# HGRN's value tiles: 32x32 block transposes on VectorE and a pass through DRAM in place of TensorE transposes

## The chip, the cores and the metric

One core of a Trainium2 chip runs the whole layer. The metric is device time in microseconds (us); the kernel before took 2657.88 us (median of three runs, 2653.09 to 2657.88). One more execution was recorded by the hardware profiler; all rows below are from that one.

## The reference

A hybrid decoder layer in float32 on 2048 tokens of width 1024. One projection feeds two groups of heads, HGRN2 (4 heads of 128) and RWKV-7 (8 heads of 64); their outputs go through one output projection, and a convolutional feed-forward follows.

```
h = rmsnorm(x)
hg_p, rw_p = split(h @ w_in)
q, f, v, g = split(hg_p, 4)          # HGRN2; v is what this change handles
f = lb + (1 - lb) * sigmoid(f);  q = silu(q) * 128**-0.5;  k = 1 - f
S_t = diag(f_t) S_{t-1} + k_t v_t^T;  o_t = S_t^T q_t
o_hg = rmsnorm_per_head(o) * norm_w * silu(g)
o_rw = rwkv7(rw_p)                   # S_t = S diag(w) + (S a) b^T + v k^T
x = x + concat(o_hg, o_rw) @ w_out
x = x + conv_ffn(rmsnorm(x))         # up, causal conv of width 3, silu gate, down
out = rmsnorm(x)
```

## The kernel before

The tokens are cut into four blocks of 512. The first stage (`phase1`) does the projections and both recurrences of all blocks; the second, which the change does not touch, does the last output projection and the feed-forward.

Everything in the first stage is kept with features on the 128 partitions and tokens along the free axis. A projection is 24 matmuls of 128x128 by 128x512 (each product of split operands takes three) into one of two `pj` banks, and an `ev_` function takes it out of the bank. For HGRN, `ev_q`, `ev_f`, `ev_v` and `ev_g` do so for a head `j` of block `nb`; there are 16 such units, (block, head). `ev_v` copies the bank with ScalarE into `hv` (two buffers): value features on partitions, 512 tokens along the row.

`hg_unit` then does the recurrence of a unit in chunks. It needs the values the other way round, tokens on partitions: `VT`, 128 x 4 x 128 with one buffer. Before, four TensorE transposes (L950) put the 128x128 blocks of `hv` into an `hg` bank and ScalarE copied them to `VT`. VT is read late in the unit: by the state update (L1053) and by the output (L1062). After that its buffer is used for a split half of the squared output (`part`).

RWKV works in `rw_super`, twice per block, on two pairs of heads. It makes products `M` (masked on VectorE at L733), stores the diagonal 32x32 blocks of them to DRAM in runs of 32 floats (`Ed`, L745), loads them back with one small matrix per partition (`E`, L748), and solves the triangular systems with a loop of 31 steps of two VectorE instructions (L800 and L802). The result `Ti` is turned with VectorE's block transpose (`TZ`, L806), and the matmuls at L819 take it up. This is called a solve below; there are eight.

The order of the work comes from three generators that are run in turn: one step of `rw_stream`, one step of `hg_stream`, then projection matmuls (`dense`) worth 2000 ns by the generator's own count. Each `yield` ends a step. The scheduler then settles each engine's order. On each engine instructions run in that order, and what an engine waits for holds up all that stands behind. SyncE issues the loads of x, the stores of oT, x1d and h2d, and RWKV's Ed and E; GpSimd issues the weights.

## Time and profile before

| | us |
|---|---|
| median of three runs | 2657.88 |
| lowest, highest | 2653.09, 2657.88 |
| the profiled execution | 2662.58 |
| its span, first to last instruction | 2660.8 |
| the first stage in it, from the first projections to the last output projection of block 2 | 30 to 1326 |

How to read the rows: PE is TensorE, PEld its weight loads, DVE VectorE, ACT ScalarE, POOL GpSimd, SP SyncE. A row of a group names line, engine, operation, output<-inputs, shape and count, then the busy time, the mean length of one in ns, the idle time of the engine just before and what ended it. A row of waits reads "who <- for whom: us in total, times, longest". A row of the timeline has start, length, engine, line, operation.

### The profile page before, as it was taken

The numbers are of one execution on the slowest core, as the hardware profiler recorded it, in microseconds if no ns is written. First come the engines' busy times: TensorE is split into PE (matmuls) and PEld (weight loads), VectorE is DVE, ScalarE is ACT, GpSimd is POOL, SyncE is SP. The second block draws the span as 40 slices with busy tenths as digits, with TensorE's granted clock in tenths as the row PEclk, the third lists the DMA queues.
The fourth block names the chain that finished last, engine by engine and source line by source line (L and its number), as shares of the span: only waits on it lengthen the run. The fifth ranks groups of instructions, "written<-read, shape, count | busy, mean of one in ns | idle before, by whom it ended". The sixth has DMA issues, their size and how long they took to land. (4 is left out here: it accounts for less than half of the span.)

```text
span 2660.8 us, 51050 instructions
## 1 busy us (share of the span) xinstructions
PE 2560.2 (96%) x19595; PEld 2061.2 (77%) x19595; DVE 1952.9 (73%) x3728; ACT 1389.2 (52%) x2274; POOL 380.4 (14%) x686
## 2 busy tenths in 40 slices
PE   7999999989999999999899999999999999999998
PEld 5777777766777777777678888887888887888887
DVE  4877667576567765767678789987998887766556
ACT  5566453545535555445456754456545544545444
POOL 6433222212222122222100000000000000000000
PEclk9999999999999999999999999999999999999999
DMA  8645443445643456744493468646763553998665
GB/s 303 204 165 170 158 143 120 130 148 203 199 143 126 156 196 199 276 131 136 154 309 113 143 204 266 233 154 225 245 203 131 166 189 127 327 320 286 197 191 186
DMA packets 312714, 510.59 MB, mean 192 GB/s; under 512 B 46879, under 2 KB 143509, under 8 KB 312469
## 3 DMA queue, kind: packets, MB, share of 16 engines
q1 hardware_dynamic: 257937, 328.99, 37.4%
q0 software_dynamic: 54464, 178.32, 20.4%
q8 instruction: 154, 2.52, 0.4%
q14 instruction: 91, 0.75, 0.1%
q10 hardware_dynamic: 68, 0.02, 0.0%
HBM read 372.99 MB, written 134.22 MB: 191 GB/s over the span
## 5 line engine op out<-in xcount | busy, mean ns | idle before, releaser
L270 PE MATMUL pj<-hh,wh 128*128 128x512 f32 x960 | 393.4, 410 | 6.2 <-ACT rkv L122 3.3
L271 PE MATMUL pj<-hl,wh 128*128 128x512 f32 x960 | 377.8, 394 | 1.3 <-issue 1.3
L272 PE MATMUL pj<-hh,wl 128*128 128x512 f32 x960 | 377.5, 393 | 0.0
L270 PE MATMUL ua<-Bh,uwh 128*128 128x512 f32 x704 | 276.4, 393 | 4.4 <-ACT m L122 3.1
L272 PE MATMUL ua<-Bh,uwl 128*128 128x512 f32 x704 | 274.6, 390 | 0.0
L271 PE MATMUL ua<-Bl,uwh 128*128 128x512 f32 x704 | 274.3, 390 | 0.0
L270 PEld LDWEIGHTS pj<-hh,wh 128*128 128x128 f32 x960 | 181.5, 189 | 55.2 <-issue 8.7
L272 PEld LDWEIGHTS pj<-hh,wl 128*128 128x128 f32 x960 | 181.1, 189 | 40.6 <-issue 1.7
L271 PEld LDWEIGHTS pj<-hl,wh 128*128 128x128 f32 x960 | 181.6, 189 | 34.3 <-DVE hl L488 0.5
L254 ACT CAST uwh<-uraw 128x512 fp32r<-128x512 f32 x220 | 134.2, 617 | 128.9 <-PE ua L271 55.7
L255 DVE TENSOR_TENSOR dal<-draw,dah 128x512 fp32r<-128x512 f32 x138 | 95.4, 691 | 113.4 <-ACT dah L254 113.2
L255 DVE TENSOR_TENSOR uwl<-uraw,uwh 128x512 fp32r<-128x512 f32 x220 | 147.6, 688 | 34.9 <-ACT uwh L254 34.8
L254 ACT CAST dah<-draw 128x512 fp32r<-128x512 f32 x138 | 85.7, 621 | 164.9 <-PE da L271 80.6
L270 PEld LDWEIGHTS ua<-Bh,uwh 128*128 128x128 f32 x704 | 132.2, 188 | 34.1 <-ACT m L122 5.7
L272 PEld LDWEIGHTS ua<-Bh,uwl 128*128 128x128 f32 x704 | 132.3, 188 | 28.1 <-DVE uwl L255 0.4
L271 PEld LDWEIGHTS ua<-Bl,uwh 128*128 128x128 f32 x704 | 132.3, 188 | 26.7
L270 PE MATMUL ud<-Bh,uwh 128*128 128x512 f32 x352 | 138.1, 392 | 0.0
L272 PE MATMUL ud<-Bh,uwl 128*128 128x512 f32 x352 | 137.2, 390 | 0.0
L271 PE MATMUL ud<-Bl,uwh 128*128 128x512 f32 x352 | 137.1, 390 | 0.0
L1493 POOL DMA_DIRECT2D gd<-y x2 | 1.1, 540 | 946.8 <-DVE y L1491 946.8
L271 PE MATMUL da<-dbl,dah 128*128 128x512 f32 x332 | 129.5, 390 | 0.2 <-DVE dbl L255 0.2
L272 PE MATMUL da<-dbh,dal 128*128 128x512 f32 x332 | 129.3, 389 | 0.0
(584 smaller groups left out, 6233.9 us busy)
## 6 DMA issues: line engine op xcount, KB each, us to landing
uraw<-in_w_up_dram SPq DMA_DIRECT2D x176, 256.0 KB, 3.1
woraw<-in_w_out_dram POOLq DMA_DIRECT2D x96, 256.0 KB, 3.6
br<-gd SPq DMA_DIRECT2D x88, 256.0 KB, 4.2
draw<-Sg SPq DMA_DIRECT2D x88, 256.0 KB, 3.3
draw<-Tw SPq DMA_DIRECT2D x88, 256.0 KB, 4.0
gd<-y SPq DMA_DIRECT2D x86, 256.0 KB, 2.9
Sg<-br SPq DMA_DIRECT2D x72, 256.0 KB, 2.1
xt<-x1d SPq DMA_DIRECT2D x32, 512.0 KB, 6.7
```

Source lines behind the costliest of these rows:

```text
L254: S.copy(hi, src)
L255: V.tensor_sub(lo, src, hi.bitcast(F32))
L270: TE.matmul(acc, lh, rh, start=first, stop=False, skip_group_check=skip)
L271: TE.matmul(acc, lh, rl, start=False, stop=False, skip_group_check=skip)
L272: TE.matmul(acc, ll, rh, start=False, stop=last, skip_group_check=skip)
L1493: (dma if end is None else nc.gpsimd.dma_start)(gd_[2 * h + b][fb * P:(fb + 1) * P, :], ys[0][:, b * BLK:(b + 1) * BLK])
```

## The change

`ev_v` no longer copies the bank. VectorE's block transpose reads it and writes `hv`: in each group of 32 partitions, each block of 32 tokens is turned in place, so a partition then holds, for every 32-token block, one token's 32 features. Four DMAs on SyncE's queue, one for each group of 32 partitions (32 features), write these runs of 32 floats into a DRAM tile `vd` (512 tokens x 128 features, three buffers) in token order. `hg_unit` loads `VT` from it with one DMA on the same queue, in place of the transposes and the copy. The `yield` behind them goes, so a unit has one step less.

```diff
         def ev_v(nb, j):
             def f(acc):
                 t_ = stg("hv", "hv", 2)
-                act(t_, acc, AF.Copy)
-                stage[("v", nb, j)] = t_
+                V.transpose(t_, acc)
+                tv = t_.rearrange("p (n c) -> p n c", c=32)
+                vd = stage[("v", nb, j)] = dp.tile([BLK, P], F32, tag="vd", name="vd", bufs=3)
+                for g in range(4):
+                    dma(vd[:, 32 * g:32 * g + 32].rearrange("(n p) c -> p n c", p=32), tv[32 * g:32 * g + 32])
             return f
...
             VT = rp.tile([P, 4, P], F32, tag="VT", name="VT")
-            tp = bank("hg")
-            for b in range(4):
-                TE.transpose(tp[:, b * P:(b + 1) * P], v[:, b * P:(b + 1) * P], ident)
-            act(VT, tp.rearrange("p (b t) -> p b t", t=P), AF.Copy)
-            yield
+            dma(VT, v.rearrange("(b p) c -> p b c", p=P))
             A = rp.tile([P, 4, 32], F32, tag="hA", name="A")
```

From here on the lines of the new kernel lie three further down between the two places, and one further up behind the second.

Where it moves instructions, at three places of the second solve (block 0, heads of the second half) and its units.

On VectorE, in the middle of the loop. Before (etmp and Ti are the loop, hf, hX and Sf belong to the HGRN unit before):

```order
L963 TENSOR_TENSOR hX<-hq,hf 128x8x32
L802 TENSOR_TENSOR Ti<-Ti,etmp 128x19x7
L969 TENSOR_TENSOR hX<-hk,Sf 128x8x32
L800 TENSOR_TENSOR etmp<-E,Ti 128x126
L970 TENSOR_TENSOR Sf<-Sf,hf 128x8x32
L802 TENSOR_TENSOR Ti<-Ti,etmp 128x18x7
L972 TENSOR_TENSOR hf<-hf 128x8x32
L800 TENSOR_TENSOR etmp<-E,Ti 128x136
L802 TENSOR_TENSOR Ti<-Ti,etmp 128x17x8
L800 TENSOR_TENSOR etmp<-E,Ti 128x128
L802 TENSOR_TENSOR Ti<-Ti,etmp 128x16x8
```

Now, at the same steps of the loop:

```order
L968 TENSOR_TENSOR hX<-hk,Sf 128x4x64
L805 TENSOR_TENSOR Ti<-Ti,etmp 128x18x7
L1001 COPY_PREDICATED A<-cst,hg 128x8x8
L803 TENSOR_TENSOR etmp<-E,Ti 128x136
L1001 COPY_PREDICATED A<-cst,hg 128x4x16
L805 TENSOR_TENSOR Ti<-Ti,etmp 128x17x8
L969 TENSOR_TENSOR Sf<-Sf,hf 128x4x64
L803 TENSOR_TENSOR etmp<-E,Ti 128x128
L361 STREAM_TRANSPOSE hv<-pj 128x512
L805 TENSOR_TENSOR Ti<-Ti,etmp 128x16x8
```

The transpose of the next unit's values now stands in the loop, and the HGRN unit is further on at the same step.

On TensorE, ahead of the solve's matmuls (pj is a projection; part belongs to the HGRN unit). Before:

```order
L1081 MATMUL hg<-part,ones 128x512
L271 MATMUL pj<-hl,wh 128x512
L272 MATMUL pj<-hh,wl 128x512
L1082 MATMUL hg<-part,ones 128x512
L270 MATMUL pj<-hh,wh 128x512
L271 MATMUL pj<-hl,wh 128x512
L272 MATMUL pj<-hh,wl 128x512
L270 MATMUL pj<-hh,wh 128x512
L271 MATMUL pj<-hl,wh 128x512
L272 MATMUL pj<-hh,wl 128x512
L819 MATMUL rw<-TZ,M 32x32 x32
```

Now:

```order
L272 MATMUL pj<-hh,wl 128x512
L270 MATMUL pj<-hh,wh 128x512
L271 MATMUL pj<-hl,wh 128x512
L272 MATMUL pj<-hh,wl 128x512
L270 MATMUL pj<-hh,wh 128x512
L271 MATMUL pj<-hl,wh 128x512
L272 MATMUL pj<-hh,wl 128x512
L822 MATMUL rw<-TZ,M 32x32 x32
```

HGRN's two matmuls stand further ahead, and the solve's come 12 projection matmuls later than before (765 since the start against 753).

On SyncE, from the first stores of oT to the second pair of loads of E. Before:

```order
L1076 DMA oT_143<-osq 128x512
L937 DMA oT_143<-yo 128x2x512
L1076 DMA oT_143<-osq 128x512
L745 DMA Ed<-M 32x16x32 x4
L748 DMA E<-Ed 64x1024 x2
```

Now:

```order
L1075 DMA oT_143<-osq 128x512 x2
L940 DMA oT_143<-yo 128x2x512
L365 DMA vd<-hv 32x16x32 x4
L748 DMA Ed<-M 32x16x32 x4
L951 DMA VT<-vd 128x4x128
L751 DMA E<-Ed 64x1024 x2
```

The unit's four stores have come ahead of Ed, and its load of VT between Ed and E.

## The prediction

> **What bounds the kernel now.** I read the page first, then the stage sums, then TensorE's waits in the changed stage.

> ```profile
> PE 2560.2 (96%) x19595; PEld 2061.2 (77%) x19595; DVE 1952.9 (73%) x3728; ACT 1389.2 (52%) x2274; POOL 380.4 (14%) x686
> 30.00:1326.00 1296.00, 1229.93 (x13736) 968.52 (x13735) 881.61 (x2096) 663.47 (x1096) 346.24 (x622) 0.99 0.52 171
> 1326.00:2661.00 1335.00, 1315.82 (x5802) 1081.98 (x5801) 1056.61 (x1597) 708.53 (x1143) 15.81 (x29) 1.00 0.64 211
> ```

> In the window rows the columns after the length are the busy times of TensorE, its weight loads, VectorE, ScalarE and GpSimd, then granted clock, DMA share and GB/s. The change lies wholly in the first stage (the 16 evictions of HGRN's values begin between 84.3 and 1229.6 us, quoted below). TensorE is busy for 1230 of its 1296 us, so it sets the time, and what is taken off it is gained if its 66 us of idle do not grow. Where that idle comes from:

> ```profile
> PE rw L865 <- ACT M L122: 6.8, 7, 2.1
> PE pj L270 <- ACT hh L247: 6.4, 7, 1.4
> PE hg L1063 <- DVE SH L1055: 5.1, 3, 4.1
> PE hg L1042 <- DVE hk L1035: 5.0, 5, 1.6
> PE rw L832 <- ACT ZT L122: 3.3, 5, 1.4
> PE rw L819 <- DVE TZ L806: 2.3, 3, 1.0
> ```

> Many short waits, no long one: TensorE's order is filled with projection matmuls, and it stops only where a chain through VectorE or ScalarE arrives just too late. The one to watch is the solve of RWKV (a loop of 31 steps on VectorE, then the transpose TZ, then matmuls at L819). In the second of the eight solves:

> ```profile
> 284.20 1.06 DVE L806 STREAM_TRANSPOSE TZ<-Ti 128x512 f32<-128x512 f32 x1
> ...
> 285.08 0.39 PE L272 MATMUL pj<-hh,wl 128*128 128x512 f32 x1
> ...
> 285.40 0.75 PE L819 MATMUL rw<-TZ,M 32*32 32x32 f32 x64
> ...
> 251.00:285.00 34.00, 32.42 (x356) 26.30 (x357) 32.61 (x111) 15.38 (x30) 10.37 (x20) 1.00 0.51 172
> ```

> VectorE is busy for 32.6 of the 34 us of this loop. TZ ends at 285.26 and L819 begins at 285.40: 0.1 us to spare. In the third:

> ```profile
> 417.30 1.08 DVE L806 STREAM_TRANSPOSE TZ<-Ti 128x512 f32<-128x512 f32 x1
> ...
> 424.40 0.75 PE L819 MATMUL rw<-TZ,M 32*32 32x32 f32 x64
> ```

> There 6.0 us are spare. The other six, read in the same way from the timeline, have 0.6, none (TensorE waits 0.9), 0.1, none (1.0), none (0.4) and 0.6.

> **What the change removes.** Four transposes per unit, with one eviction on ScalarE.

> ```profile
> 97.06 0.60 PE L950 MATMUL hg<-ident,hv 128*128 128x128 f32 x4
> 97.42 0.48 PE L270 MATMUL pj<-hh,wh 128*128 128x512 f32 x1
> ...
> 1252.69 0.66 PE L950 MATMUL hg<-ident,hv 128*128 128x128 f32 x4
> 1253.10 0.48 PE L270 MATMUL pj<-wh,ohl 128*128 128x512 f32 x1
> ...
> L950 PE MATMUL hg<-ident,hv x64: 270/273/421, 97.1 to 1253.1; 128*128 128x128 f32 x64
> L122 ACT ACTIVATE hv<-pj x16: 587/598/600, 84.3 to 1229.6; 128x512 f32<-128x512 f32 x16
> ...
>   PE pj L272: 48.4, 12
> ...
> L1053 PE MATMUL hg<-VT,KT x128: 270/275/377, 130.8 to 1298.0; 128*128 128x128 f32 x128
> L122 ACT ACTIVATE VT<-hg x16: 594/597/607, 98.2 to 1254.4; 128x512 f32<-128x512 f32 x16
> ```

> Matmuls overlap, so what counts is from the first transpose to the next matmul: 97.42 − 97.06 = 0.36 us in the first unit, 0.41 in the last. The 13 of 16 groups with nothing between the four have 0.35 to 0.51, on average 0.38; 16 x 0.38 = **6.1 us** off TensorE. ScalarE loses 16 x (0.60 + 0.60) = 19 us, and no longer stands 48 us waiting for the projection. It is half idle; only its waits above could shrink. I count nothing, with a bound of 3 us gained.

> **What it adds on VectorE.** 16 block transposes out of a bank. The trace has none that reads a bank; its nearest rows:

> ```profile
> L812 DVE STREAM_TRANSPOSE TTs<-TZ 32x512 f32<-32x512 f32 x32 | 22.5, 703 | 0.8
> L806 DVE STREAM_TRANSPOSE TZ<-Ti 128x512 f32<-128x512 f32 x8 | 8.4, 1055 | 0.2
> L1075 DVE TENSOR_TENSOR osq<-osq,hgg 128x512 f32<-128x512 f32 x16 | 11.0, 685 | 0.1
> L1074 DVE TENSOR_TENSOR osq<-hg,osq 128x512 f32<-128x512 f32 x16 | 10.9, 682 | 12.5 <-ACT osq L122 12.5
> L314 DVE SCALAR_TENSOR_TENSOR rkv<-lastc,vt,rkv 128x1 f32<-128x1 f32 x48 | 10.1, 210 | 0.0
> L315 DVE COPY lastc<-pj 128x1 f32<-128x1 f32 x56 | 8.5, 152 | 1.1
> L956 DVE MEMSET Sf<- 128x256 f32 x15 | 4.1, 272 | 2.6 <-PE hg L1081 2.3
> ...
> 264.92 0.60 ACT L122 ACTIVATE hv<-pj 128x512 f32<-128x512 f32 x1 [4.55 <-PE pj L272]
> 265.88 0.29 DVE L800 TENSOR_TENSOR etmp<-E,Ti 128x128 f32<-128x128 f32 x1
> ```

> Between 0.70 and 1.06 us each; I take 1.06, the row with the same 128 x 512. The transposes of even units (0, 2, ...) come just before or among the masks of M (L733), where VectorE waits for TensorE anyway (10.9 us in 7 waits, below): nothing, and 8 x 1.06 = 8.5 us if that cover is gone. Those of odd units fall into the solves, where the rest of the loop is queued behind them. In the second, the product of 128 elements that stands just ahead of the transpose in the new order ran at 265.88, and the projection was done by 264.92: VectorE comes to it after TensorE, so the price is its length and no wait. But other work of the unit moves into the solves with it, since a unit now has one step less and runs ahead by one to two steps. In the second solve the order has six more instructions ahead of TZ: the transpose and one each of L956, L1074, L1075, L314 and L315, 1.06 + 0.27 + 0.68 + 0.69 + 0.21 + 0.15 = 3.1 us. TensorE's order has 12 more projection matmuls ahead of the solve's matmuls there (0.23 us each, 285.08 − 284.86 apart in the timeline) and four transposes less: 12 x 0.23 − 0.38 = 2.4 us. TZ is thus late by 3.1 − 2.4 = 0.7 against TensorE, of which 0.1 is spare: 0.6 us of new wait. Counted in the same way, VectorE's part in the eight solves grows by 2.4, 3.1, 2.1, 3.1, 2.6, 3.7, −3.6 and 3.8 us, TensorE's by 0.1, 2.4, −0.4, 2.8, 1.7, 3.4, −3.2 and 1.9 (instructions more or less in each, by the mean of their group). Less what is spare that leaves 1.7, 0.6, 0, 0.3, 0.8, 0.3, −0.4 and 1.3: **4.6 us** of new wait.

> **What it adds on the queues.** SyncE issues five more DMAs per unit, 80 in all: four stores of 64 KB in runs of 128 bytes, then a load of 256 KB. Nearest rows:

> ```profile
> E<-Ed SPq DMA_DIRECT2D x16, 256.0 KB, 3.1
> Ed<-M SPq DMA_DIRECT2D x32, 64.0 KB, 3.3
> ...
> SPq L745 <- DVE M L733: 214.4, 5, 97.1
> SPq L748 <- DMA Ed<-M: 25.1, 14, 3.0
> ...
> DVE etmp L800 <- DMA E<-Ed: 19.8, 5, 5.7
> DVE M L733 <- PE rw L730: 10.9, 7, 3.8
> ```

> Store and load take 3.3 + 3.1 us and a little issue, some 8 us, where the old way had VT ready 98.8 − 97.1 = 1.7 us after its start; but VT is first read 32 us after its eviction (98.2 against 130.8), so nobody waits. The load waits at the head of SyncE's queue for its stores and, VT having one buffer, for the unit before. Behind it stand in the second solve the two loads of E, on which VectorE's loop waits. They wait for Ed's stores anyway (25.1 us in 14 waits), and the unit's stores went out before those: I count nothing. Elsewhere stores of oT, loads of x or of oraw stand behind it. GpSimd's queue with the weights gets nothing new.

> [...]

> Sum: −6.1 + 4.6 = **−1.5 us**. The profiled execution took 2662.58 us (its span of 2660.8 and 1.8 around it), 0.2% above the median of 2657.88. Against its own time that gives 2661.1, on the median 2656.4.

> **The rivals.** *The solves take it all up* (faster): if TZ keeps pace, or the waits that ScalarE causes shrink by 3 us, the change brings 6.1 to 9.1 us, 2649 to 2652. For it: four of eight solves have their matmuls 10 to 12 projection matmuls later, and DVE's L1055 and L1035, which TensorE waits for 10 us in all, are done earlier. Against it: only one solve has over 1 us to spare.

> *VectorE becomes the bound* (slower): the chain from the masks of M to TZ runs on VectorE with hardly a gap. If the even transposes cost their 8.5 us too, the sum is −1.5 + 8.5 = +7.0, 2665. It decides for slower once the even ones cost over 0.85 us each (8 x 0.85 = 6.8 = 1.5 + 5.3). For it: spare of 0.1 us; against it: the 10.9 us that VectorE stands before M. [...]

> *E comes late* (slower): the load of VT gets between Ed and E and shares the queue. Each E late by up to 3.1 us in seven solves with no slack is 7 x 3.1 = 22 us, at half of that 11: −1.5 + 11 = +9.5, 2667. It decides from 1.0 us per solve. Against it: the two are issued together and E's issue waits longer for Ed than VT's for its stores.

> *The change doesn't take TensorE's work away*: the order has no transposes of hv left, so I give that nothing.

> **How the numbers follow.** My forecast, a change within 0.2%, gets 0.41; faster 0.34; VectorE as the bound 0.13, E late 0.12. A measurement of this kernel can tell about 0.2%, 5.3 us, from no change. The forecast alone spans 2653 to 2663. The range for 8 in 10 takes in the other cases: low 2646, the 9.1 us gain and 3 us for the scatter of the runs before (2653.09 to 2657.88); high 2668, the dearer of the slow rivals.

> **What would show it.** No matmul from hv, and TensorE's busy time in the first stage 5 to 7 us lower; its wait for TZ up from 2.3 to about 7 us. Wrong would be: transposes of hv beyond 1.2 us; VectorE's wait for E well over 19.8 us (E late); TensorE waiting for VT by DMA; the wait for M at L733 unchanged while VectorE's idle falls (even units not hidden); or a gain beyond 10 us, which would mean that ScalarE's 48 us before hv had cost TensorE something.

## The result, and the profile after

| | before | after |
|---|---|---|
| median of the runs, us | 2657.88 | 2674.35 |
| lowest, highest | 2653.09, 2658.74 | 2672.33, 2676.36 |
| the profiled execution | 2662.58 | 2672.78 |
| its span | 2660.8 | 2671.0 |
| first stage in it, from 30 us to the last projection | to 1325.6 | to 1333.8 |

The ratio is 1.0057, with a 95% interval of 1.0042 to 1.0071: slower by 0.6%, and above the range of 2646 to 2668. The two profiled executions lie only 10.2 us apart, the medians 16.5, so the traces can account for the first of these and not for the other 6 us. Two executions of all that follow, one in experiment e14 (4179.94 us, granted clock 0.558) and one of the kernel before (2830.50 us, 0.85), were slow as a whole and are left out.

The rows of the changed kernel that answer to those shown of before: the page's busy times, then the windows of the two stages (length, busy times of TensorE, its weight loads, VectorE, ScalarE and GpSimd, granted clock, DMA share, GB/s).

```profile
PE 2557.3 (96%) x19531; PEld 2051.7 (77%) x19531; DVE 1958.5 (73%) x3744; ACT 1386.1 (52%) x2252; POOL 381.0 (14%) x686
30.00:1334.00 1304.00, 1227.12 (x13677) 960.27 (x13675) 886.26 (x2110) 659.81 (x1071) 348.07 (x624) 0.99 0.56 177
1334.00:2671.00 1337.00, 1316.81 (x5803) 1081.62 (x5802) 1058.68 (x1599) 709.20 (x1146) 15.80 (x29) 1.00 0.64 210
```

TensorE has 64 matmuls less and in its first stage it is 2.8 us less busy (1229.93 before). But its idle time there grew from 1296 − 1229.93 = 66.1 us to 1304 − 1227.12 = 76.9. What ends that idle time, in TensorE's waits of the first stage, first before and then after; only the rows called "issue" are shown, and of after those of the solve and of the three largest others:

```profile
PE hg L988 <- issue: 2.4, 2, 2.1
PE pj L271 <- issue: 1.7, 2, 1.3
PE pj L270 <- issue: 1.4, 1, 1.4
```

```profile
PE hg L987 <- issue: 11.1, 8, 2.1
PE pj L270 <- ACT hh L247: 8.8, 7, 2.6
PE hg L1041 <- DVE hk L1034: 5.9, 6, 3.2
PE rw L868 <- ACT M L122: 4.5, 7, 1.3
...
PE rw L868 <- issue: 2.3, 1, 2.3
PE rw L882 <- issue: 2.0, 1, 2.0
...
PE rw L822 <- DVE TZ L809: 0.9, 3, 0.4
...
PE pj L270 <- issue: 0.5, 1, 0.5
...
PE rw L848 <- issue: 0.4, 1, 0.4
```

"issue" is time in which the engine waited for nothing that the profile shows. Before rounding these rows add up to 5.5 us before and 16.4 after: 10.9 us more, as much as the idle time grew. Summed in the same way, what ends with VectorE is 26.7 us in both, with ScalarE 31.4 and 31.9, with a DMA nothing in either. The wait for TZ, where the prediction put 4.6 us, fell from 2.3 to 0.9.

The new operations themselves, and VectorE's waits that the prediction watched:

```profile
L361 DVE STREAM_TRANSPOSE hv<-pj x16: 705/709/717, 85.9 to 1241.3; 128x512 f32<-128x512 f32 x16
...
vd<-hv SPq DMA_DIRECT2D x64, 64.0 KB, 3.3
VT<-vd SPq DMA_DIRECT2D x16, 256.0 KB, 3.4
...
DVE etmp L803 <- DMA E<-Ed: 10.7, 5, 4.0
DVE M L736 <- PE rw L733: 4.6, 6, 2.4
...
DVE hv L361 <- PE pj L272: 2.7, 2, 2.0
```

A block transpose out of a bank took 0.71 us, and what stores and loads its result is about as long as expected (3.3 and 3.4 us, against 3.3 and 3.1). The wait for E fell from 19.8 to 10.7 us. So none of the rivals is what happened, and the loss is in a wait that no rival named.

**What those stalls have in common.** The changed kernel has twelve of 0.4 us or more, all in the first stage, eleven of them at the short matmuls of HGRN and RWKV. Here is TensorE's timeline round the third; a group of equal matmuls is one row, and the bracket is the idle time before it.

```profile
396.82 0.40 PE L272 MATMUL pj<-hh,wl 128*128 128x512 f32 x1
397.15 1.58 PE L783 MATMUL rw<-UV,M 64*64 64x64 f32 x64
398.66 0.46 PE L987 MATMUL hg<-hq,hk 128*32 128x32 f32 x32
398.93 0.94 PE L987 MATMUL hg<-hX 128*32 128x16 f32 x84
401.80 0.31 PE L987 MATMUL hg<-hX 128*32 128x16 f32 x12 [1.94 <-issue]
```

TensorE stops in the middle of a group, 12 matmuls before its end, and the profile shows nothing that it waits for. Other such stops:

```profile
166.73 0.54 PE L987 MATMUL hg<-hX 128*32 128x16 f32 x42 [1.65 <-issue]
310.64 1.38 PE L868 MATMUL rw<-UV,KBT 128*64 128x64 f32 x39 [2.31 <-issue]
798.39 0.43 PE L987 MATMUL hg<-hX 128*32 128x16 f32 x27 [2.09 <-issue]
```

Counting TensorE's records in the trace (matmuls, weight loads and its few semaphore instructions), there are 3072 = 12 x 256 from the stop at 166.73 to that at 310.64, then 2048 = 8 x 256 to the one at 401.80, then 8704 = 34 x 256 to 798.39. And of the DMA queues that the page calls "instruction" one fits that number:

```profile
q8 instruction: 153, 2.51, 0.4%
```

All 18 traces of this case, those of the experiments below included, agree with the reading. Taken in order, each packet can be paired with one place where TensorE goes over into a new page (a page mark in what follows), 2750 pairs in all. None of these marks is passed sooner than 1.19 us after its packet has ended. In the first stages there are 102 waits called issue. Of these 87 stand at a mark, and each ends 1.2 to 1.6 us after the mark's packet. The other 15 all stand before a projection matmul of L270 and fit no packet (0.5 of the 16.4 us here, 1.5 of the 5.5 before); what they are is open, and the sums of issue below include them.

### The profile page after: what moved, and what is told of

It is laid out like the page before. It is cut to its first block, busy times and chain, and to the rows that moved or that the text cites. A ratio compares the mean times of both kernels' runs of the same rounds, so it can differ in the third digit from the quotient of the medians.

```text
span 2671.0 us, 51060 instructions
## 1 busy us (share of the span) xinstructions
PE 2557.3 (96%) x19531; PEld 2051.7 (77%) x19531; DVE 1958.5 (73%) x3744; ACT 1386.1 (52%) x2252; POOL 381.0 (14%) x686
## 4 chain that ended last, share of the span: by engine, by line
PE 64%; DVE 13%; issue 8%; DMA 7%; ACT 6%; POOL 1%; SPq 0%; DVEq 0%; POOLq 0%; ACTq 0%
PE pj L270 6%; PE pj L272 5%; PE pj L271 5%; PE ua L270 4%; PE ua L272 4%; PE ua L271 4%; PE da L271 3%; PE da L270 3%; PE da L272 3%; PE ud L272 2%; PE ud L271 2%; PE ud L270 2%; PE db L271 2%; PE db L270 2%; PE db L272 2%
## 5 line engine op out<-in xcount | busy, mean ns | idle before, releaser
L270 PE MATMUL pj<-hh,wh 128*128 128x512 f32 x960 | 393.7, 410 | 1.7 <-DVE xh L416 0.9
L272 PE MATMUL pj<-hh,wl 128*128 128x512 f32 x960 | 377.7, 394 | 0.0
L270 PE MATMUL ua<-Bh,uwh 128*128 128x512 f32 x704 | 276.6, 393 | 4.2 <-ACT m L122 3.9
L272 PE MATMUL ua<-Bh,uwl 128*128 128x512 f32 x704 | 274.4, 390 | 0.0
L270 PEld LDWEIGHTS pj<-hh,wh 128*128 128x128 f32 x960 | 181.0, 189 | 53.5 <-issue 12.0
L272 PEld LDWEIGHTS pj<-hh,wl 128*128 128x128 f32 x960 | 181.1, 189 | 40.0 <-issue 0.7
L270 PEld LDWEIGHTS ua<-Bh,uwh 128*128 128x128 f32 x704 | 132.1, 188 | 35.4 <-ACT m L122 8.1
L272 PEld LDWEIGHTS ua<-Bh,uwl 128*128 128x128 f32 x704 | 132.1, 188 | 28.0 <-DVE uwl L255 0.4
L271 PEld LDWEIGHTS ua<-Bl,uwh 128*128 128x128 f32 x704 | 132.2, 188 | 26.7
L270 PE MATMUL ud<-Bh,uwh 128*128 128x512 f32 x352 | 138.0, 392 | 0.0
L272 PE MATMUL ud<-Bh,uwl 128*128 128x512 f32 x352 | 137.1, 389 | 0.0
L272 PE MATMUL da<-dbh,dal 128*128 128x512 f32 x332 | 129.2, 389 | 0.0
## 6 DMA issues: line engine op xcount, KB each, us to landing
uraw<-in_w_up_dram SPq DMA_DIRECT2D x176, 256.0 KB, 3.2
woraw<-in_w_out_dram POOLq DMA_DIRECT2D x96, 256.0 KB, 3.5
br<-gd SPq DMA_DIRECT2D x88, 256.0 KB, 4.0
draw<-Sg SPq DMA_DIRECT2D x88, 256.0 KB, 2.8
draw<-Tw SPq DMA_DIRECT2D x88, 256.0 KB, 4.1
gd<-y SPq DMA_DIRECT2D x86, 256.0 KB, 2.9
Sg<-br SPq DMA_DIRECT2D x72, 256.0 KB, 2.2
```

Of the source, the lines that this page charges most:

```text
L270: TE.matmul(acc, lh, rh, start=first, stop=False, skip_group_check=skip)
L271: TE.matmul(acc, lh, rl, start=False, stop=False, skip_group_check=skip)
L272: TE.matmul(acc, ll, rh, start=False, stop=last, skip_group_check=skip)
```

## The experiments

The theory to test, called F below: the loss is these stalls, and their number depends on where the runs of short matmuls fall in the pages. The change removes 64 matmuls with their loads and a step of the unit, so it moves both the code against the pages and the work against other work. The rivals: the new route costs something itself (VectorE, DMAs), the missing step makes the order worse in another way, or the runs differ at their start.

To move code against the pages alone, tiny transposes of 32x32 are put ahead of the program, into TensorE's wait for its first operands (11.3 us in the changed kernel). Each is two TensorE instructions, a matmul and its weight load, nothing reads them, and from some 25 us on the order on every engine stays as it was.

```diff
-        vps = pst("vps")
+        vps = pst("vps"); [TE.transpose(vps[0:32, P:P + 32], ident[0:32, 0:32], ident[0:32, 0:32]) for _ in range(N)]
```

In the tables, "ahead" is the number of TensorE instructions added (2 N), "issue" the sum of the waits of that name in the first stage of the profiled execution, the time is the median, and the ratio is to the kernel before on the same chip. The runs were on several chips, on which the kernel before had medians of 2657.73 to 2660.76; so the ratios compare better than the times. Issue comes from one execution, the time from 4 to 12.

### The parts of the change, one at a time

e1: the changed kernel with the step put back, so that only the route of the values is new.

```diff
             dma(VT, v.rearrange("(b p) c -> p b c", p=P))
+            yield
```

> The changed kernel with the yield behind VT's load put back, so that the steps are those of before and only the route of the values is changed. If the missing step (the work running ahead) is the cause of the +15 us, this falls to 2650 to 2660. If the route is (VectorE's transposes, the DMAs), it stays at 2670 to 2677. If the cause is where TensorE's runs of short matmuls fall in the 256-instruction pages in which its code is fetched, the time follows the idle before TensorE that the profile calls issue: about 2654 plus what that sum is above 5.5 us (before: 5.5 us in the first stage, after: 16.4).

e2: the kernel before without the step, so that TensorE still makes the transposes.

```diff
             act(VT, tp.rearrange("p (b t) -> p b t", t=P), AF.Copy)
-            yield
```

> The kernel before without the yield behind its TensorE transposes, which stay. If the missing step is the cause: 2668 to 2677. If the route is: 2653 to 2661. If the pages are: 2657 plus what TensorE's idle called issue is above 5.5 us in the first stage.

| | issue, us | time, us | ratio, 95% |
|---|---|---|---|
| before | 5.5 | 2657.88 | |
| after | 16.4 | 2674.35 | 1.0057, 1.0042 to 1.0071 |
| e1, route alone | 0.6 | 2642.54 | 0.9939, 0.9924 to 0.9953 |
| e2, missing step alone | 14.4 | 2670.08 | 1.0041, 1.0027 to 1.0056 |

The new route gains; the missing step loses. Neither time is what the pages alone would give: e1 was forecast at about 2649 us by them and at 2650 or more by the other theories, and took 2642.5; e2 was forecast at 2666 by them and took 2670.1. e1's first stage:

```profile
30.00:1306.00 1276.00, 1222.06 (x13662) 959.63 (x13662) 884.65 (x2110) 645.49 (x1061) 346.54 (x621) 0.99 0.56 180
```

Its idle time is 1276 − 1222.06 = 53.9 us, 23.0 less than the changed kernel's, and 15.8 of these are issue. That the step's loss is one of pages is not shown by this.

### Only the place in the pages moved

> The changed kernel with 72 transposes of 32x32 (144 TensorE instructions) ahead of everything, while TensorE waits for its first data; from 30 us on every engine's order is the same as in the changed kernel. Pages: counted over the changed kernel's trace, this shift leaves the fewest runs of 256 instructions that pass in under 3 us; idle called issue falls from 16.4 to 4 to 9 us, the time by 7 to 12 us to 2662 to 2667. Route or step: no change but for the start, 2672 to 2678.

> The kernel before with 12 such transposes (24 TensorE instructions) ahead of everything; order unchanged from 30 us on. Pages: this shift puts the most runs badly; idle called issue rises from 5.5 to 9 to 15 us and the time by 3 to 9 us, to 2661 to 2667. Route or step: no change, 2653 to 2660.

> The kernel before without its step (e2) took 2670.1 us, with 10 stalls called issue of together 14.4 us in its first stage. Here 44 transposes of 32x32 (88 TensorE instructions) stand ahead of it in the wait at the start, so that the same instructions, in the same order on TensorE from 25 us on, fall elsewhere in the 256-instruction pages of its code. Theory F (a page not yet there when a run of short matmuls ends it): issue falls to 3 to 7 us, the time by 6 to 12 us, to 2658 to 2664, as slow as the kernel before or nearly: then the missing step costs nothing by itself. Rival S (the missing step itself is dear, since the order of the work round the recurrence is worse without it): the time stays within 3 us of 2670, whatever issue does.

> The changed kernel with its step put back (e1) took 2642.5 us with 0.6 us of issue. Here 108 transposes of 32x32 (216 TensorE instructions) stand at its start. Theory F, by the spacing of the page marks in e1: issue rises to 6 to 12 us, and the time by 6 to 12, to 2648 to 2655. Rival S (e1 is fast because of its order): 2640 to 2645, issue under 3.

> The kernel before with 72 transposes of 32x32 (144 TensorE instructions) at its start, as e3 had them for the changed kernel. Theory F, by the spacing of the marks in the kernel before: issue 7 to 12 us (5.5 before), time 2659 to 2666. Rival W (what made e3 21 us faster than the changed kernel is the 144 instructions at the start themselves, an earlier start or a warmer engine, and not where the pages fall): this kernel gains the same 15 to 22 us, to 2638 to 2645.

> The changed kernel with 128 transposes of 32x32 at its start: 256 TensorE instructions, one whole page of code, so that every later instruction keeps its place within its page. Theory F: the stalls of the changed kernel are back at the same places, issue 13 to 18 us (16.4 there, 2.8 with 144 instructions), time 2668 to 2675, less what is gained at the very start (1 to 4 us). Rival W (any instructions at the start do it): 2650 to 2656 as with 144, issue under 6.

| | ahead | issue, us | time, us | ratio, 95% |
|---|---|---|---|---|
| e3, after | 144 | 2.8 | 2652.85 | 0.9974, 0.9961 to 0.9987 |
| e8, after | 256 | 13.8 | 2672.27 | 1.0051, 1.0032 to 1.0069 |
| e5, before without step | 88 | 3.2 | 2655.48 | 0.9995, 0.9983 to 1.0007 |
| e4, before | 24 | 5.2 | 2660.04 | 1.0005, 0.9995 to 1.0016 |
| e7, before | 144 | 1.4 | 2657.02 | 0.9994, 0.9984 to 1.0005 |
| e6, route alone | 216 | 1.3 | 2647.19 | 0.9953, 0.9941 to 0.9966 |

With 144 instructions ahead the changed kernel loses nearly all its stalls and is 21.5 us faster, below the kernel before. With 256 ahead, one page, they are back, at the same instructions. e8's timeline at two of them (the changed kernel's rows above have x84, then x12 behind the stall, and x42 behind that at 166.73):

```profile
391.12 0.94 PE L987 MATMUL hg<-hX 128*32 128x16 f32 x85
393.93 0.30 PE L987 MATMUL hg<-hX 128*32 128x16 f32 x11 [1.88 <-issue]
...
159.35 0.54 PE L987 MATMUL hg<-hX 128*32 128x16 f32 x41 [2.12 <-issue]
```

Each stop lies one matmul further on than in the changed kernel: a page later within one matmul. The same group in e3, whole:

```profile
384.50 1.58 PE L783 MATMUL rw<-UV,M 64*64 64x64 f32 x64
386.01 0.46 PE L987 MATMUL hg<-hq,hk 128*32 128x32 f32 x32
386.29 1.03 PE L987 MATMUL hg<-hX 128*32 128x16 f32 x96
```

That rules out that any instructions at the start do it, which e7 confirms: the same 72 transposes that bring the changed kernel 21.5 us bring the kernel before hardly anything. One thing there is not as the theory has it: e7 has 4.1 us less of issue than the kernel before, but its ratio is a gain of 0.06% (1.6 us), at most 0.16%. Not all of the 21.5 us is stalls either: these are 13.6, and the projections begin 2.2 us earlier (19.12 against 21.34, though without any transposes ahead they begin anywhere from 18.92, in e1, to 21.49, in e9). The remaining 6 us are not settled. The granted clock may have a part in them: its mean over the runs is 0.992 in the changed kernel, 0.993 in e3 and 0.990 in e8, and among the runs of one kernel 0.001 less of it goes with some 2 us more (0.2 to 2.9 in the sixteen experiments).

e5 speaks against a cost of the missing step by itself: at another place the kernel without it takes 2655.5, no more than the kernel before (0.9983 to 1.0007).

The forecasts of how much each place would stall missed three times. They were worked out from how closely the page marks follow each other, and gave issue of 9 to 15 us for e4, 6 to 12 for e6 and 7 to 12 for e7, where 5.2, 1.3 and 1.4 were measured. The times of e3 and e5 missed too, 9 and 3 us below their ranges (2662 to 2667 and 2658 to 2664): moving the code gained more than the stalls counted. So where the marks lie is shown, but closeness alone doesn't tell which of them stall (more on this at the end).

### The shift in the middle

e9: the changed kernel with the 72 transposes in the ninth HGRN unit, into a bank that its short matmuls use next.

```diff
-            l1 = bank("hg")
+            l1 = bank("hg"); [TE.transpose(l1[0:32, 0:32], ident[0:32, 0:32], ident[0:32, 0:32]) for _ in range(72 * ((nb, j) == (2, 0)))]
```

> The changed kernel with the 72 transposes of 32x32 (144 TensorE instructions, 4.0 us in e3) not at its start but in the ninth of the 16 HGRN units, at about 744 us, where TensorE is busy. Theory F: what stands ahead keeps its place in the pages, what stands behind is shifted as in e3. So the seven stalls of the changed kernel up to 672 us stay (9.2 us together there), and of the five behind (7.1 us) at most 2 us are left; issue 9 to 12 us. Time: 4 us of added transposes, less 5 to 10 us of stalls and what follows them: 2666 to 2673. Rival W (it was the instructions at the start): all twelve stalls stay, issue 15 to 18, time 2676 to 2680.

2662.91 us, ratio 1.0015 (1.0001 to 1.0028): 11.4 us less than the changed kernel, with 4 us of transposes more. In the trace these lie at 641 to 656 us, spread between projections and earlier than expected, but within one stretch without stalls. e9's waits called issue from 30 to 640 us:

```profile
PE hg L987 <- issue: 6.8, 4, 2.1
PE rw L868 <- issue: 2.4, 1, 2.4
```

From 640 us to the end of the stage there is no such row at all, where the changed kernel has four:

```profile
PE hg L987 <- issue: 4.7, 3, 2.1
PE rw L882 <- issue: 2.0, 1, 2.0
PE pj L270 <- issue: 0.5, 1, 0.5
PE rw L848 <- issue: 0.4, 1, 0.4
```

The five stalls of over 1 us ahead of the shift stand where they stood, those behind it are gone. The time fell below the forecast of 2666 to 2673.

### Unlucky place, or a kernel prone to stalls?

Left was whether the step just happened to move the code to a bad place. So the changed kernel, and the one with its step put back, ran at evenly spread places.

> The changed kernel with its step put back (e1), and 12 transposes of 32x32 (24 TensorE instructions) at its start, the place that the spacing of e1's page marks names as the best: issue under 1.5 us. Theory F: 2638 to 2645, like e1, since e1 has nearly nothing left to lose. If the spread between placements has another cause than the stalls, the time may lie anywhere from 2640 to 2660 with issue still under 1.5.

> The changed kernel with 24 transposes of 32x32 (48 TensorE instructions) at its start. So far the kernels without the step had 14 to 16 us of issue in two places of the pages and 3 in two others; those with it 0.5 to 5.5 in six. Theory P (only the place in the pages decides, the step just happened to shift it): over five places spread evenly (0, 48, 96, 144, 192) the changed kernel's issue ranges from under 4 to over 12 and the kernel with the step put back does the same over six places. Theory S (without the step the runs of short matmuls stand closer, so more marks are met in too short a time): the changed kernel's mean is 8 us or more, that with the step stays under 4 at each place. Time at this place: 2650 + 1.5 x issue.

> The changed kernel with 48 transposes of 32x32 (96 TensorE instructions) at its start, the third of five places. Theories P and S as for 48. By either, time 2650 + 1.5 x issue; if issue is under 4 here and at 48 and 192, the place 0 was merely unlucky and theory P alone holds.

> The changed kernel with 96 transposes of 32x32 (192 TensorE instructions) at its start, the last of five even places; 0, 48, 96 and 144 gave 16.4, 9.1, 4.8 and 2.8 us of issue. If exposure changes gradually with the place, 192 lies between 144 and 256 (13.8): 5 to 11 us, time 2655 to 2667. Theory S then has a mean of 8 us or more over the five, as it asked.

> The changed kernel with its step put back and 36 transposes of 32x32 (72 TensorE instructions) at its start; 0, 24 and 216 gave 0.6, 0.5 and 1.3 us of issue. Theory P: a bad place is still to be found, at 72, 120 or 168, with 6 us or more and a time of 2654 or more. Theory S: under 4 us and 2642 to 2652 here too.

> The changed kernel with its step put back and 60 transposes of 32x32 (120 TensorE instructions) at its start. Theories P and S as for 72: a bad place with 6 us or more and 2654 or more by P, under 4 us and 2642 to 2652 by S.

> The changed kernel with its step put back and 84 transposes of 32x32 (168 TensorE instructions) at its start, the sixth place; 0, 24, 72, 120 and 216 gave 0.6, 0.5, 2.8, 2.4 and 1.3 us. Theory S: under 4 us and 2644 to 2656. Theory P: 6 us or more and 2656 or more.

| | ahead | issue, us | time, us | ratio, 95% |
|---|---|---|---|---|
| after | 0 | 16.4 | 2674.35 | 1.0057, 1.0042 to 1.0071 |
| e11 | 48 | 9.1 | 2664.88 | 1.0025, 1.0012 to 1.0038 |
| e12 | 96 | 4.8 | 2657.11 | 0.9995, 0.9980 to 1.0011 |
| e3 | 144 | 2.8 | 2652.85 | 0.9974, 0.9961 to 0.9987 |
| e13 | 192 | 8.8 | 2665.09 | 1.0006, 0.9991 to 1.0022 |
| e1, step kept | 0 | 0.6 | 2642.54 | 0.9939, 0.9924 to 0.9953 |
| e10, step kept | 24 | 0.5 | 2650.15 | 0.9951, 0.9933 to 0.9969 |
| e14, step kept | 72 | 2.8 | 2656.00 | 0.9988, 0.9972 to 1.0003 |
| e15, step kept | 120 | 2.4 | 2652.51 | 0.9986, 0.9968 to 1.0003 |
| e16, step kept | 168 | 1.0 | 2648.40 | 0.9950, 0.9935 to 0.9966 |
| e6, step kept | 216 | 1.3 | 2647.19 | 0.9953, 0.9941 to 0.9966 |

Without the step the mean over the places is 8.4 us of issue, with it 1.4, and no bad place was found for it. Both theories hold their half: the place sets how much a kernel stalls, and the missing step makes it prone. By the 2650 + 1.5 x issue of the expectations the times of e11 and e12, and of e13 reckoned likewise, come out within 2 us. e10, e14 and e15 took 5, 4 and 0.5 us more than theory allowed, with 0.5, 2.8 and 2.4 us of issue: the kernels with the step differ by 13 us among each other for reasons that the stalls do not cover, as e10's expectation said such a time would mean.

Why the step matters shows in the order. The two groups of the stop at 401.80, RWKV's and HGRN's, as they stand in e1:

```profile
385.95 1.58 PE L783 MATMUL rw<-UV,M 64*64 64x64 f32 x64
387.46 0.50 PE L270 MATMUL pj<-hh,wh 128*128 128x512 f32 x1
...
389.44 0.39 PE L272 MATMUL pj<-hh,wl 128*128 128x512 f32 x1
389.76 0.46 PE L988 MATMUL hg<-hq,hk 128*32 128x32 f32 x32
390.03 1.03 PE L988 MATMUL hg<-hX 128*32 128x16 f32 x96
```

Nine projection matmuls, 2.3 us, lie between RWKV's 64 short matmuls and HGRN's 128; the kernel before has the same nine (its L780 at 390.20, its L988 at 393.97). In the changed kernel the two groups touch: 192 matmuls with 192 loads, one and a half pages, pass in 2.8 us where nothing stalls (e3's rows above). A step of a unit brings a turn of projection matmuls with it, and without the step the unit's short matmuls come a turn earlier. Over the whole first stage, with the stalls taken out of the times, the share of stretches of 384 TensorE instructions that pass in under 5.25 us is 1.0% in the kernel before, 1.1% in e7, 1.0% in e1 and 0.9% in e6 and e16; without the step it is 4.1% in the changed kernel, 4.7% in e3, 3.8% in e11, 5.9% in e2 and 6.6% in e5. The place in the pages does not change this share, the step does. The bound of 5.25 us was chosen afterwards; by stretches of 256 in under 3.2 us it is 4.2% in every kernel with the step and 5.5 to 8.5% without it, a smaller contrast the same way round. Nor is the share all: the kernel before has the same as e1 and stalls for 5.5, 5.2 and 1.4 us at its three places.

The fastest version run is e1, the new route with its step, at 0.6% under the kernel before (0.9924 to 0.9953); at six places the same kernel has ratios of 0.9939 to 0.9988, on average 0.996.

## Why the prediction was wrong

**What bounds the kernel** was read right but not to the end. TensorE does set the time. "It stops only where a chain through VectorE or ScalarE arrives just too late" was wrong: 5.5 of the 66 us of the kernel before were called issue already, in three rows that the prediction left out, and these grew.

**What the change removes**, −6.1 us off TensorE, fits the route alone. e7 and e1 both keep the step and hardly stall; e7's first stage:

```profile
30.00:1319.00 1289.00, 1227.97 (x13733) 968.62 (x13731) 881.16 (x2096) 662.78 (x1095) 347.74 (x622) 0.99 0.53 172
```

1227.97 − 1222.06 = 5.9 us less busy. In the changed kernel it is only 2.8 (1229.93 − 1227.12), short of the 5 to 7 that the prediction asked for. But one pair of executions can't settle this: at e1's six places the same work took from 1218.2 to 1226.4 us. On average it is 1229.4 us over the three places of the kernel before, 1222.8 over the six of the new route with its step, and 1225.5 over the five of the changed kernel: 6.6 and 3.9 us less. The 3 us that ScalarE might have given at most don't show: TensorE's waits that end with ScalarE average 30.0 us over those three places and 30.8 over the six.

**What it adds on VectorE** was too dear. The transpose took 0.71 us, the lower bound, and 1.06 had been taken. Those of the even units were hidden as said: VectorE's wait for M fell by 10.9 − 4.6 = 6.3 us, about the 8 x 0.71 = 5.7 that they take.

**The step that failed** is the one that worked out what the missing step of the unit does: "other work of the unit moves into the solves with it, since a unit now has one step less", priced at **4.6 us** of new wait for TZ. That wait fell by 1.4 us, from 2.3 to 0.9; it is 0.8 to 0.9 at all five places of the changed kernel and 0.8 at the six with the step kept, so with the new route the step does not move it. The missing step does cost, but on TensorE: it brings short matmuls next to short matmuls, and where a page mark falls there, TensorE can stop, by the reading above for its code. In the run as predicted that is 10.9 us more; averaged over five places it is 8.4 against 5.5, 5.2 and 1.4 at the three places of the kernel before. The prediction took the order of TensorE only as a count of matmuls ahead of the solve (765 against 753) and never looked at how close its short ones stand, nor at a resource that depends on the number of instructions ahead. No rival held this case.

**The queues** were read right: nobody waits for VT by a DMA, and E was not late, its wait fell from 19.8 to 10.7 us. So the slow rival "E comes late" is out, and so is "VectorE becomes the bound", for which the even units would have had to cost their time; e1, with the transposes on VectorE, is 0.6% faster than the kernel before. The wrong sign that the prediction named at the other end, a gain of over 10 us, came up too, in e1 (15.3 us; the six places average 0.4%, about 10 us); by the waits above ScalarE had no visible part in it.

Taken over the places, the sum of −1.5 us was not far off: the ratios of the changed kernel at its five places run from 0.9974 to 1.0057 with a mean of 1.001. The forecast was for one place, and that was the worst of the five. That the average comes near −1.5 us is luck: the wait for TZ of 4.6 us in that sum didn't come, and stalls that it didn't have took its place.

## What to carry to other kernels

Read the rows of TensorE called "issue" with the others: where they come in the middle of a group of short matmuls, count TensorE's instructions between them; here it was a multiple of 256 (3072, 2048, 8704), and the stalls are read as late code. Then an edit that only takes instructions away, or that lets two groups of short matmuls touch, can cost more than it removes, as here: 10.9 us more of these stalls against 2.8 us less of TensorE's work. Keep long matmuls between such groups (with the step, which put nine there in the rows above, 0.5 to 5.5 us of issue at nine places; without it, 2.8 to 16.4 at eight), and compare a change at several places in the pages (a few dozen unused instructions ahead of the program; the changed kernel took 2652.85 to 2674.35 us over its five) before it is judged by some tenths of a per cent.

## What the runs showed of the hardware

- The stops that are read as a late page of TensorE's code lasted 0.15 to 2.6 us, and TensorE went on 1.2 to 1.6 us after the mark's packet had ended (87 stops in 18 traces, 41 of them over 1 us). These stops lie at the same number within the page, 193 or 194 of 256 by the trace's records.
- Pages came about one ahead. In the first stages a page's packet started in the median 0.7 us after the page before it was entered, and lasted 1.0 us. With the 1.2 us behind it, the least that was seen, a page that passes in under some 3 us is at risk (an estimate from these three figures). Packets did not start evenly, though: nine in ten lay between 3.1 us before that point and 2.7 us after it. In e7 one page passed in 1.24 us without a stall at its end: the packet for the next had started 3.5 us before that page was entered. What makes a packet early or late is open.
- Whole runs of one kernel spread by more than the differences in question, and along with the granted clock: e8's six runs go from 2663.52 us at a mean clock of 0.993 to 2679.96 at 0.988. One run of each can't settle differences of some tenths of a per cent.
- VectorE's block transpose of 128 x 512 out of a bank took 0.71 us, where the one of the same size for TZ, out of another tile, took 1.06 in the kernel before and 1.08 in the changed one; why is not tested.
